# Row sums of a 32 x 512 x 1024 tensor: each load of 16 rows split into a transfer of the even and one of the odd partitions

## Chip, cores, metric

One core of one Trainium2 chip, alone. The metric is device time in microseconds (us), median of several executions.

## The reference

```python
x = np.random.randn(32, 512, 1024).astype(np.float32)   # 67.11 MB
out = np.sum(x, axis=-1).astype(np.float32)             # 16,384 sums
```

## The kernel before

The 16,384 rows are laid out as two blocks, of 112 and of 16 rows for each of the 128 partitions. A tile has 16 rows a partition (128 x 16384 elements), in one of three buffers. VectorE sums a tile in one reduction. SP issues the loads. Seven tiles come from the first block; the second block is cut ever finer (9, 4, 2 rows and one row in two pieces), so that little is left to do when its last bytes land. There, and in the last tile of the first block (7 of its 16 rows), ACT takes part of the rows.

```python
xpool = ctx.enter_context(tc.tile_pool(name="x", bufs=3))
...
        while c < whole:
            m = min(G, whole - c)                       # G = 16
            xt = xpool.tile([P, G * D], F32, tag="xt", name="xt")
            parts = (0, 1, m) if done + c == 0 else (0, m)   # the very first row alone
            for i, k in zip(parts, parts[1:]):
                nc.sync.dma_start(
                    out=xt[:, i * D : k * D], in_=x_b[:, (c + i) * D : (c + k) * D]
                )
            a = ACT_ROWS if done + c + m == full else 0
            rows_dve(xt, res, 0, m - a, c)
            rows_act(xt, res, m - a, a, c + m - a)
            c += m
        if not final:

            for i, k in ((0, 104), (104, P)):
                nc.scalar.dma_start(out=out_b[i:k], in_=res[i:k])
...
    cuts = [0, 9, 13, 15]                               # the last block
    for i, k in zip(cuts, cuts[1:]):
        nc.sync.dma_start(out=xt[:, i * D : k * D], in_=x_b[:, (c + i) * D : (c + k) * D])
```

After compiling, the first `EARLY` loads are moved ahead of the program's starting barrier. (Cuts are marked by "...".)

## Time and profile before

| | before |
|---|---|
| time, median | 162.3 us at first (3 runs); 161.96 to 162.23 in later batches |
| span of the profiled core | 160.4 us |
| VectorE busy | 121.4 us (76%) |
| ACT busy | 17.2 us (11%) |
| DMA engines | 67.18 MB, 419 GB/s over the span |

The two busy shares suggest that no compute engine sets the time; the stretches in the prediction show that the DMA engines do (share 1.00 at 435 GB/s). For the end of the kernel, which the change also touches, here are lines of the timeline of before (start, duration, engine, line, operation, and in brackets the idle time ahead and what ended it):

```profile
147.72 0.99 ACTq L99 DMA_DIRECT2D out_dram<-res  x2
149.07 1.06 ACT L55 ACTIVATE xt<-xt 128x1024 f32<-128x1024 f32 x1 [2.45 <-DMA xt<-in_x_dram]
...
157.48 0.19 ACT L55 ACTIVATION_READ_ACCUMULATOR xt<-xt 128x1 f32 x1
...
158.18 0.35 SPq L128 DMA_DIRECT2D out_dram<-res  x1
```

ACT issues two stores, waits for the nine rows of the last block, and is done 0.5 us before the last store of all is issued.

### The profile page before, as it was taken

The numbers are of one execution on the slowest core, as the hardware profiler recorded it, in microseconds if no ns is written. First come the engines' busy times: TensorE is split into PE (matmuls) and PEld (weight loads), VectorE is DVE, ScalarE is ACT, GpSimd is POOL, SyncE is SP. The second block draws the span as 40 slices with busy tenths as digits, with TensorE's granted clock in tenths as the row PEclk, the third lists the DMA queues.
The fourth block names the chain that finished last, engine by engine and source line by source line (L and its number), as shares of the span: only waits on it lengthen the run. The fifth ranks groups of instructions, "written<-read, shape, count | busy, mean of one in ns | idle before, by whom it ended". The sixth has DMA issues, their size and how long they took to land.

```text
span 160.4 us, 122 instructions
## 1 busy us (share of the span) xinstructions
DVE 121.4 (76%) x17; ACT 17.2 (11%) x31; POOL 0.2 (0%) x4
## 2 busy tenths in 40 slices
DVE  0000059997799959999499994999949998698883
ACT  0000000000000000000000000000000000695892
POOL 0000000000000000000000000000000000000000
DMA  9988996996996996996996996997998999998992
GB/s 376 490 368 368 490 523 261 523 523 261 523 523 261 523 523 261 523 523 261 523 507 278 523 490 294 523 474 310 523 425 359 523 392 392 441 395 369 431 393 79
DMA packets 2169, 67.18 MB, mean 419 GB/s; under 512 B 505, under 2 KB 633, under 8 KB 889
## 3 DMA queue, kind: packets, MB, share of 16 engines
q1 hardware_dynamic: 2016, 67.12, 97.4%
q10 hardware_dynamic: 153, 0.06, 0.1%
HBM read 67.11 MB, written 0.07 MB: 419 GB/s over the span
## 4 chain that ended last, share of the span: by engine, by line
DMA 75%; DVE 22%; SPq 0%; issue 0%; DVEq 0%
DMA xt<-in_x_dram 75%; DVE res L47 21%; DVE pairs L67 1%; SPq L105 0%; DVE seen L123 0%; DVE tail L67 0%; DVEq L136 0%; DVE res L67 0%
## 5 line engine op out<-in xcount | busy, mean ns | idle before, releaser
L47 DVE TENSOR_REDUCE res<-xt 128x16 f32<-128x16384 f32 (+3 forms) x9 | 119.8, 13308 | 35.1 <-DMA xt<-in_x_dram 35.1
L55 ACT ACT_TABLE_LOAD x1 | 1.3, 1283 | 137.9 <-DMA xt<-in_x_dram 137.9
L55 ACT ACTIVATE xt<-xt 128x1024 f32<-128x1024 f32 x15 | 15.6, 1043 | 2.5 <-DMA xt<-in_x_dram 2.5
L55 ACT ACTIVATION_READ_ACCUMULATOR xt<-xt 128x1 f32 x15 | 2.8, 186 | 0.0
L42 DVE MEMSET tail<- 128x1 f32 x1 | 0.1, 59 | 1.3 <-PEq L173 1.3
L67 DVE CUSTOM_DVE_ANT_0 pairs<-xt 128x512 f32<-128x512 f32 x1 | 0.7, 692 | 0.3 <-DMA xt<-in_x_dram 0.3
L67 DVE CUSTOM_DVE_ANT_0 pairs<-tail 128x272 f32<-128x272 f32 (+1 forms) x2 | 0.9, 426 | 0.0
L123 DVE COPY seen<-tail 128x2 f32<-128x2 f32 x1 | 0.2, 168 | 0.0
L67 DVE DVE_READ_ACCUMULATOR2_ANT res<- 128x1 f32 x2 | 0.2, 82 | 0.0
L173 POOL MEMSET const-bfloat16-1.0<- 128x1 bf16 x1 | 0.1, 103 | 0.0
L173 POOL MEMSET const-uint8-127<- 128x1 uint8 x1 | 0.1, 102 | 0.0
L173 POOL MEMSET const-float32-1.0<- 128x1 f32 x1 | 0.1, 100 | 0.0
L173 POOL MEMSET const-float32-0.0<- 128x1 f32 x1 | 0.1, 99 | 0.2 <-issue 0.2
L67 DVE DVE_READ_ACCUMULATOR2_ANT tail<- 128x1 f32 x1 | 0.1, 80 | 0.0
## 6 DMA issues: line engine op xcount, KB each, us to landing
xt<-in_x_dram SPq DMA_DIRECT2D x1, 7680.0 KB
xt<-in_x_dram SPq DMA_DIRECT2D x1, 4608.0 KB, 32.6
xt<-in_x_dram SPq DMA_DIRECT2D x1, 2048.0 KB, 37.1
xt<-in_x_dram SPq DMA_DIRECT2D x1, 1024.0 KB, 39.2
xt<-in_x_dram SPq DMA_DIRECT2D x1, 512.0 KB, 3.6
tail<-in_x_dram SPq DMA_DIRECT2D x1, 272.0 KB, 39.3
tail<-in_x_dram SPq DMA_DIRECT2D x1, 240.0 KB, 39.2
xt<-in_x_dram SPq DMA_DIRECT2D x6, 40.8
```

The lines of the kernel that those rows point to most:

```text
L42: nc.vector.memset(tail[:, CUT + 15 : CUT + 16], 0.0)
L47: nc.vector.tensor_reduce(out=res[:, c : c + n], in_=xt[:, j * D : (j + n) * D].rearrange("p (j d) -> p j d", d=D), axis=X, op=ADD,)
L55: return nc.scalar.activation(out=v, in_=v, func=COPY, accum_out=acc)
L67: nc.vector.tensor_tensor_reduce(out=pairs[:, 0 : h - a], in0=v[:, a:h], in1=v[:, h:b], scale=1.0, scalar=0.0, op0=ADD, op1=ADD, accum_out ...
L123: nc.vector.tensor_copy(out=seen, in_=tail[:, CUT + 14 : CUT + 16])
L173: nc = _bacc.Bacc("TRN2", target_bir_lowering=False, num_devices=1)
```

## The change

Its visible intent: more and smaller transfers, so that a second one is always queued behind the first. Stores of the first block's results become three and stand behind the last loads; three loads are issued ahead of the barrier instead of two.

```diff
-EARLY = 2
+EARLY = 3
@@
-            parts = (0, 1, m) if done + c == 0 else (0, m)
-            for i, k in zip(parts, parts[1:]):
+            parts = [(q, 0, m) for q in (slice(0, P, 2), slice(1, P, 2))]
+            if done + c == 0:
+                parts = [(slice(0, P), 0, 1)] + [(q, 1, m) for q, i, k in parts]
+            for q, i, k in parts:
                 nc.sync.dma_start(
-                    out=xt[:, i * D : k * D], in_=x_b[:, (c + i) * D : (c + k) * D]
+                    out=xt[q, i * D : k * D], in_=x_b[q, (c + i) * D : (c + k) * D]
                 )
@@
         if not final:
-
-            for i, k in ((0, 104), (104, P)):
-                nc.scalar.dma_start(out=out_b[i:k], in_=res[i:k])
+            out_a, res_a = out_b, res
@@ behind the last loads
+    for i, k in ((0, 104), (104, 116), (116, P)):
+        nc.scalar.dma_start(out=out_a[i:k], in_=res_a[i:k])
```

## The prediction

Rival 1, "the clash", is that splitting a tile by partitions slows its packets; no trace of before has a transfer of 64 partitions that lie two apart, and the prediction called this the whole risk. Its figures stand as estimates, from the supposition of half the rate and from the trace: twice 2418 ns is 4.8 us, the 134 us of the split part come a second time (about 296 us in all), half of 435 GB/s is near 220, and half a tile of 19.34 us is the 9.7 that takes the range to 172 us. ("For this" there means a harmless split.) Rival 3 was a fixed cost of every transfer, which the prediction held to be hidden, from the spacing of 19.34 us.

> **What bounds the kernel now.** I read the page's chain of work that ended last first, then its DMA rows, then the windows by stage, then the queue's own waits.
>
> The chain of the kernel before:
>
> ```profile
> DMA 75%; DVE 22%; SPq 0%; issue 0%; DVEq 0%
> DMA xt<-in_x_dram 75%; DVE res L47 21%; DVE pairs L67 1%; SPq L105 0%; DVE seen L123 0%; DVE tail L67 0%; DVEq L136 0%; DVE res L67 0%
> ```
>
> Three quarters of the chain are loads. The 21% of VectorE are two reductions that the chain follows because a later load waits for a buffer which they free. Whether that wait costs time is decided by whether the DMA engines run dry during it. The page's slices of DMA, busy tenths and GB/s, seem to say that they do:
>
> ```profile
> DMA  9988996996996996996996996997998999998992
> GB/s 376 490 368 368 490 523 261 523 523 261 523 523 261 523 523 261 523 523 261 523 507 278 523 490 294 523 474 310 523 425 359 523 392 392 441 395 369 431 393 79
> ```
>
> A 6 after every two 9s looks like a hole at each transfer's end. It is none. A slice is 160.4/40 = 4.01 us. One row of a tile is 16 x 4096 = 65,536 bytes, one packet; the trace's packet records give it a median of 2418 ns, on 16 engines almost in step. So a slice is charged with either one round of packets (16 x 65,536 / 4.01 us = 261 GB/s) or two (523). 523, 523, 261 has the mean 436. The windows by stage, cut where the reductions start, give it without that artefact (columns: stretch and its length, busy us of DVE, ACT and POOL, clock, DMA share, GB/s):
>
> ```profile
> 0.00:2.50 2.50, 0.06 (x1) 0.00 (x0) 0.20 (x4) 1.00 0.55 139
> 21.80:41.10 19.30, 17.22 (x1) 0.00 (x0) 0.00 (x0) 1.00 1.00 435
> 60.50:79.80 19.30, 17.20 (x1) 0.00 (x0) 0.00 (x0) 1.00 1.00 435
> 99.20:118.50 19.30, 17.20 (x1) 0.00 (x0) 0.00 (x0) 1.00 1.01 435
> 137.90:149.10 11.20, 9.76 (x2) 8.69 (x16) 0.00 (x0) 1.00 0.97 408
> 149.10:157.70 8.60, 7.83 (x7) 8.51 (x16) 0.00 (x0) 1.00 0.92 382
> 157.70:160.40 2.70, 0.46 (x3) 0.00 (x0) 0.00 (x0) 1.00 0.03 3
> ```
>
> In the middle the engines have no hole: share 1.00. A tile of 16 rows is 8 packets on each engine, 8 x 2.418 = 19.34 us, and the reductions start 19.3 us apart (21.84, 41.13, 60.48, 79.82, 99.18, 118.53, 137.88 in the timeline). VectorE needs 17.22 of those 19.34 us, so it has 2.1 us to spare for each tile. The kernel is bound by the rate of the 16 engines, 27.1 GB/s each.
>
> How much could any change of the loads win? 67.11 MB at 16 x 27.1 = 433.6 GB/s take 154.8 us; the span is 160.4. Outside stand the first packet's start (1.05 us), the slow first row (its packets take up to 999 ns where 159 is the median, about 1 us), slower packets in the last block (408 and 382 GB/s, about 1 us) and the end after the last landing (2.7 us). The change touches none of these; its aim, the seams between tiles, has nothing to give.
>
> The waits of the SP queue, in which the new waits will stand:
>
> ```profile
> SPq L89 <- DVE res L47: 68.9, 4, 17.3
> SPq L105 <- DVE res L47: 17.2, 1, 17.2
> SPq L105 <- DMA xt<-in_x_dram: 1.8, 1, 1.8
> ```
>
> They cost nothing: the median load needs 40.8 us from issue to landing and itself runs for 19.3, so about one whole load is queued ahead of it.
>
> [...]
>
> **The change, part by part.**
>
> *Loads.* Seven loads (six of 16 rows, one of 15) become fourteen of 64 partitions. The packets stay 65,536 (and 61,440) bytes, 128 for a tile; [...] Added are 7 completion records on each engine; the trace has 9 ns for one: 7 x 9 = 0.06 us on the path. Added are also 7 issues of SP at 328 ns (0.64 the longest): SP is idle for 19 us between loads, so only the start matters. There the third load is issued ahead of the starting barrier, while the first row is in transit; the second transfer has 4 x 2.27 = 9 us of queued work ahead of the third. Nothing on the path.
>
> *Waits.* A reduction waits for two semaphores; both halves pass the same engines one after the other, so the second half lands when the whole tile did. The last loads now wait for semaphores in use: in the compiled order the 4 rows and 2 rows wait for the two halves of tile 5 (landing about 109 and 118.5), the two last pieces for the halves of tile 6 (about 128 and 137.9). The last of these is issued at 138 and is due when the 9 + 4 + 2 rows ahead have passed, about 156.5. 18 us of slack: hidden. Before, the last piece waited for tile 5.
>
> *Stores.* The first block's results go in three transfers (104, 12, 12 partitions) instead of two. Two issues took 0.99 us on ACT's queue from 147.72; a third adds some 0.5, to 149.2, where ACT's next row could start at 149.07. ACT's tail is then up to 0.2 us later, against 0.14 us that it waits before its last row and 0.5 us between its end (157.67) and the last store (158.18): hidden. The third store seems to be there so that the loads of the tail keep their semaphores.
>
> Sum if nothing else happens: 162.3 + 0.06, with a tenth for the waits: 162.4 us.
>
> **The rivals.**
>
> [...]packets of some 4.8 us, not 2.418. For the split part (6 tiles of 19.34 us and 18.1 us, 134 us) that would be 134 us more, about 296 in all. The trace's landings are spread over just 0.56 us, at every tile the same, so engines do run in step. [...]For this speaks only that someone chose even and odd and then took care over the semaphores of the tail, which is not done around a loss of that size. I give the clash, in any form, a quarter.
>
> *2. The seams were real after all,* and a half queued behind each half closes them. Against it: share 1.00 and 19.34 us for eight packets of 2.418. Worth at most the 1 us of the first row or of the tail: 161.3.
>
> [...]
>
> **Range and chances.** Rival 3 and the main line are the same outcome, 162.3 to 162.7, with 161.6 below for luck at start and end. That takes about 0.7. The clash has 0.25, spread from 165 to 296 with no good guide to where. A range that shall hold 8 times in 10 has to take in its mild end: half a tile at half rate is 9.7 us, so up to 172. Faster by over 2% (under 159.1) would have to beat the 154.8 us of data plus the 4.8 us of start (1.05 us, and about 1 us of first row) and end (2.7 us): 0.02. Within 2%: 0.72. Slower: 0.26.
>
> **What would show each step.** Right: packets of 65,536 bytes again at 2418 ns; reductions again 19.3 us apart; the windows' DMA share 1.00 at 435 GB/s; DVE busy 121.4 us; ACT's end and last store no more than 0.3 us later. Rival 1: packets of up to 4.8 us, or in two groups, the windows near 220 GB/s at first, and landings of the 16 engines apart by several us where they were 0.56; the packets of the unsplit first row and last rows as before. Rival 2: no window changes, but the first reduction starts before 21.8. The prediction is wrong if [...]a tail load is issued after the queue has run dry, which would stand as a gap ahead of the 4-row or 2-row reductions (1.44 and 0.46 us of waiting now).

## The result, and the profile after

162.18 us (161.92 to 162.31, 4 runs) against 162.23 us for the kernel before: ratio 0.9997, with a 95% interval of 0.9979 to 1.0016. Nothing changed within noise. A ratio here and below is the mean time of one kernel's fast runs over that of the other's of the same rounds, so it is not quite the ratio of the medians.

The chain of work that ended last, after:

```profile
DMA 73%; DVE 23%; another core or an unknown queue 1%; SPq 1%; issue 0%; DVEq 0%
```

Much the same chain, with loads in front (the unknown queue is one piece of 2.07 us, which the trace does not resolve). The windows of the kernel after, cut at the same times (columns as before):

```profile
0.00:2.50 2.50, 0.06 (x1) 0.00 (x0) 0.20 (x4) 1.00 0.57 139
...
21.80:41.10 19.30, 17.22 (x1) 0.00 (x0) 0.00 (x0) 1.00 1.00 435
...
60.50:79.80 19.30, 17.22 (x1) 0.00 (x0) 0.00 (x0) 1.00 1.00 435
...
99.20:118.50 19.30, 17.22 (x1) 0.00 (x0) 0.00 (x0) 1.00 1.00 435
...
137.90:149.10 11.20, 9.90 (x2) 8.67 (x15) 0.00 (x0) 1.00 0.96 415
149.10:157.70 8.60, 7.88 (x8) 8.23 (x15) 0.00 (x0) 1.00 0.90 372
157.70:160.30 2.60, 0.30 (x2) 0.19 (x2) 0.00 (x0) 1.00 0.04 3
```

The middle is the same to the digit: 435 GB/s at share 1.00. In the trace's records of packets, the 768 packets of 65,536 bytes have the same median, 2418 ns (27.1 GB/s for each of the 16 engines), and the longest of them is 2608 (2493 before). In the same records the second half of the second tile ends 9.7 us after the first half, which is four packets of 2418 ns. The waits of the SP queue did change:

```profile
SPq L93 <- DVE res L47: 69.1, 4, 17.3
SPq L93 <- DMA xt<-in_x_dram: 19.9, 5, 9.0
...
SPq L110 <- DMA xt<-in_x_dram: 18.7, 2, 9.3
SPq L107 <- DVE res L47: 17.3, 1, 17.3
SPq L107 <- DMA xt<-in_x_dram: 2.2, 2, 1.2
```

The row with L110 has grown: the two last pieces now wait 18.7 us in all for semaphores that the halves of the last whole tile still hold, where before they waited 0.2 us (the same line of code was L108 there). Whether this matters is read from the DMA rows and not from the size of the wait: the last piece takes 19.5 us from issue to landing, because 15 rows are queued ahead of it (they had landed by 156.32). And the end of the timeline after:

```profile
147.95 1.40 ACTq L116 DMA_DIRECT2D out_dram<-res  x3
...
149.47 1.06 ACT L55 ACTIVATE xt<-xt 128x1024 f32<-128x1024 f32 x1 [2.60 <-DMA out_dram<-res]
...
157.70 0.19 ACT L55 ACTIVATION_READ_ACCUMULATOR xt<-xt 128x1 f32 x1
...
158.04 0.35 SPq L133 DMA_DIRECT2D out_dram<-res  x1
```

ACT's third store holds it up until 149.47 (149.07 before), and it is done 0.22 us later, at 157.89. That is still 0.15 us ahead of the last store, which goes out at 158.04.

One small thing moved that the prediction did not mention: the third load ahead of the barrier delays the barrier itself, so VectorE's first instruction starts at 2.31 us instead of 1.32. It then waits until 22.00 for data anyway.

### The profile page after: what moved, and what is told of

Read it like the earlier page. It is cut to its first block, busy times and chain, and to the rows that moved or that the text cites. A ratio compares the mean times of both kernels' runs of the same rounds, so it can differ in the third digit from the quotient of the medians.

```text
span 160.3 us, 138 instructions
## 1 busy us (share of the span) xinstructions
DVE 121.5 (76%) x17; ACT 17.1 (11%) x31; POOL 0.2 (0%) x4
## 2 busy tenths in 40 slices
DMA packets 2293, 67.18 MB, mean 419 GB/s; under 512 B 629, under 2 KB 757, under 8 KB 1013
## 4 chain that ended last, share of the span: by engine, by line
DMA 73%; DVE 23%; another core or an unknown queue 1%; SPq 1%; issue 0%; DVEq 0%
DMA xt<-in_x_dram 73%; DVE res L47 21%; DVE pairs L67 1%; SPq L93 1%; DVE seen L128 0%; DVEq L47 0%; DVE tail L67 0%; DVE res L67 0%; DVEq L141 0%
## 6 DMA issues: line engine op xcount, KB each, us to landing
tail<-in_x_dram SPq DMA_DIRECT2D x1, 240.0 KB, 19.5
```

## The experiments

A result of zero has several possible causes: nothing of the change acts; or a gain and a loss cancel; or the risk named in the prediction (the clash: a split by partitions slows the packets) does not exist at all; or it exists, and even and odd partitions happen to avoid it. Nine runs tell these apart. All gave the right result. The expectations name two theories. By theory A the rate depends on which partitions a transfer takes. Its packets of 4.8 us and times of about 290 us are estimates, from twice the 2418 ns of before. (In the forecast for the four transfers, its two outcomes stand one after the other: without a clash and with it.) By theory B the rate does not depend on the partitions.

### The kernel before, a second time

No edit.

> The kernel before, unchanged, for a second trace: how much of the small differences between the two traces (first reduction at 21.84 or 22.00 us, the nine-row packets at a mean of 1405 or 1365 ns, spread of the 16 engines' landings 0.56 or 0.48 us) is chance. If they belong to the change, this run repeats 21.84, 1405 and 0.56 within a few hundredths. If they are chance, at least one of them moves by as much as it did between the two traces. Time 162.2 us either way.

Measured: 162.14 us, ratio 0.9998. First reduction at 22.02 us, mean of the nine-row packets 1367 ns, landings of the 16 engines 0.59 us apart. So the differences of 0.16 us and of 40 ns between the first two traces are chance: this trace of the kernel before has the values of the changed one. The spread of the landings did not move to the changed kernel's 0.48; that it is not the change's either shows in the run with the stores alone, whose unsplit loads land within 0.43 to 0.50 us. These differences are not explained further.

### Halves instead of even and odd

```diff
-            parts = [(q, 0, m) for q in (slice(0, P, 2), slice(1, P, 2))]
+            parts = [(q, 0, m) for q in (slice(0, 64), slice(64, P))]
```

> As the changed kernel, but the two transfers take partitions 0 to 63 and 64 to 127. Theory A ([...]even/odd partitions cost nothing[...]):[...] packets slow down to at least 4.8 us and the kernel takes 290 us or more;[...] packets of up to 9.7 us, up to 560 us.[...] Theory B ([...]the 27.1 GB/s are the engines' own): packets stay at 2.42 us, 162.3 us.

Measured: 308.78 us, ratio 1.904. The windows of this run, each one tile long:

```profile
42.00:82.40 40.40, 17.18 (x1) 0.00 (x0) 0.00 (x0) 1.00 1.00 208
122.90:163.40 40.50, 17.26 (x2) 0.00 (x0) 0.00 (x0) 1.00 1.00 207
204.00:244.40 40.40, 17.14 (x1) 0.00 (x0) 0.00 (x0) 1.00 1.00 208
```

The DMA share is 1.00, as in the kernel before: all 16 engines are busy all the time, at half the rate. A share of 1.00 says that the engines hold packets, not that they move them at full speed; the GB/s beside it say that (208 here, 435 before). A packet of 65,536 bytes has a median of 5118 ns, and the 16 landings of a transfer stay 0.9 us apart, so all 16 engines take part, in step. Theory B falls: the engines move 27.1 GB/s each with even and odd partitions (65,536 bytes in 2418 ns), and 12.8 with the halves (in 5118). The very same edit with other slices nearly doubles the time, so the change did carry the risk. Theory A said this in advance, except for the size: not 4.8 us but 5.1, so a packet takes 2.1 times as long, not 2. Why it does is not shown. Packets of 9.7 us (an estimate for a worse case: four times 2418 ns) did not appear.

### Four transfers a tile

```diff
-            parts = [(q, 0, m) for q in (slice(0, P, 2), slice(1, P, 2))]
+            parts = [(slice(r, P, 4), 0, m) for r in range(4)]
```

> As the changed kernel, but four transfers a tile, of the partitions that are 0, 1, 2, 3 modulo 4. [...]packets 2.42 us, 162.4 us (14 more completion records of 9 ns are 0.13 us). [...]about 290 us in step. Theory B: 162.4 us. If a transfer has a cost of its own on the path, it shows here three times as large as in the changed kernel: over 0.5 us more would need such a cost of over 25 ns.

Measured: 162.29 us against 162.12, ratio 1.0005 (0.9988 to 1.0022), packets 2418 ns, the longest 2434. Again no clash (2418 ns in the changed kernel too), and three times as many extra transfers as in the changed kernel cost at most a few tenths of a us. A fixed cost for each transfer, if any is on the path, is too small to see here.

### Eight transfers a tile

```diff
-            parts = [(q, 0, m) for q in (slice(0, P, 2), slice(1, P, 2))]
+            parts = [(slice(r, P, 8), 0, m) for r in range(8)]
```

> As the changed kernel, but eight transfers a tile, of the partitions that are r modulo 8. [...]Theory A: packets of 4.8 us as long as the engines are in step, about 290 us; [...]Theory B: packets 2.42 us, 162.3 us plus 49 completion records of 9 ns (0.4 us).

Measured: 309.56 us, ratio 1.909, median packet 5105 ns. A window of one tile:

```profile
42.00:82.40 40.40, 17.19 (x1) 0.00 (x0) 0.00 (x0) 1.00 1.01 208
```

Split by 2 or by 4 nothing happens (2418 ns); split by 8 the rate is halved (208 GB/s for 435). So being spread is not enough: 64 partitions 2 apart and 32 that lie 4 apart run at full rate, 16 that lie 8 apart and 64 neighbours do not. The size of a transfer in bytes does not tell these runs apart: the quarter is smaller than the half and runs at full rate. What does tell them apart was not shown: theory A expected the slow packets of the halves and of the eight transfers, but from a mechanism that no record shows. In every run the rows that are read go with the partitions that are written, so not even the reading and the writing side were set apart.

### Engines put out of step

This tells whether the full rate of the even/odd transfers hangs on the engines being in step (theory A2) or not (theory A1). The first forecast is that of A1, and the second that of A2, whose 2.5 to 4.8 us are an estimate: up to twice the 2418 ns.

```diff
             if done + c == 0:
-                parts = [(slice(0, P), 0, 1)] + [(q, 1, m) for q, i, k in parts]
+                uneven = [slice(0, P, 16), slice(8, P, 16)]
+                uneven += [slice(r, P, 8) for r in (2, 4, 6)] + [slice(1, P, 2)]
+                parts = [(slice(0, P), 0, 1)] + [(q, 1, 8) for q in uneven] + [(q, 8, m) for q, i, k in parts]
```

> The changed kernel with the engines put out of step on purpose: rows 1 to 7 of the first tile come in six uneven transfers, of which the first two (8 partitions each) give packets to eight engines only; from row 8 on all is as in the changed kernel. [...]the 768 packets of 65,536 bytes stay at 2418 ns, though the 16 landings of a transfer now lie some 2 to 5 us apart, where they were 0.5. Cost only at the start and the end, 164 to 169 us. [...]packets of 2.5 to 4.8 us all through the run, and 175 us or more.

Measured: 170.47 us, ratio 1.052; a little over the stated 169, because the uneven transfers themselves run slower than I had reckoned: their packets of 28,672 bytes take a median of 2082 ns and up to 3558, where 1062 is my estimate of the undisturbed time (28,672 bytes at 36.76 ps and 8.7 ns a packet, from the packet times given with the split by rows), and the first reduction starts at 30.01 us, 8.0 later than in the changed kernel. After that nothing is lost, as three windows show:

```profile
40.00:59.40 19.40, 17.20 (x2) 0.00 (x0) 0.00 (x0) 1.00 1.00 432
79.00:98.40 19.40, 17.26 (x2) 0.00 (x0) 0.00 (x0) 1.00 1.00 432
118.00:137.40 19.40, 17.20 (x2) 0.00 (x0) 0.00 (x0) 1.00 1.00 432
```

The 16 landings now lie 1.86 us apart, a little less than the 2 to 5 expected, in two groups of eight, and stay so from the first tile to the last. The 768 packets take 2418 to 2429 ns, where theory A2 asked for 2.5 to 4.8 us. The landings inside the groups differ by up to 0.18 and 0.64 us, and no packet is stretched by more than 11 ns. So theory A2 fails, and A1 holds: out of step or in step, the packets keep their time for the length of the run. Which engine took which packets was not seen, as the packet records do not name engines.

### Eight transfers in another order

```diff
-            parts = [(q, 0, m) for q in (slice(0, P, 2), slice(1, P, 2))]
+            parts = [(slice(r, P, 8), 0, m) for r in (0, 4, 1, 5, 2, 6, 3, 7)]
```

Two outcomes were named: the clash wears off, or it stays.

> As the run with eight transfers a tile, but in the order 0, 4, 1, 5, 2, 6, 3, 7[...]. [...]packets come down to 2.42 us after some tiles and the time is 165 to 200 us. [...]packets stay near 5.1 us and the time near 309 us.

Measured: 302.5 us (one run, state unknown); the 768 packets of 65,536 bytes took 4902 to 5029 ns. The clash did not wear off. The first and the last landing of a transfer lie 2.47 us apart, half a packet, but that is one engine alone: the other 15 land within 1.00 us. I cannot say why the packets come down from 5105 to 4909 ns and no further; this stays open. None of three clashing kernels came out below 302 us. That speaks against the mild clash, for whose sake the prediction's range went up to 172 us, but only for these three splits.

### The stores alone

To the kernel before only this was done:

```diff
-            for i, k in ((0, 104), (104, P)):
-                nc.scalar.dma_start(out=out_b[i:k], in_=res[i:k])
+            out_a, res_a = out_b, res
@@ behind the last loads
+    for i, k in ((0, 104), (104, 116), (116, P)):
+        nc.scalar.dma_start(out=out_a[i:k], in_=res_a[i:k])
```

> The kernel before with nothing of the change but its stores: three transfers (104, 12, 12 partitions) issued behind the last loads. If the zero of the whole change is the sum of a gain and a loss, this part is off from 1 by itself. By the prediction it is hidden: 162.2 us, ratio 0.998 to 1.002.

Measured: 161.98 us against 161.96, ratio 0.9999 (0.9981 to 1.0016). No hidden gain or loss in this part. Its trace shows that moving the stores is enough to lengthen a wait: the two last pieces wait 19.7 us in all (0.2 before), and that too costs nothing.

### Split by rows instead of partitions

```diff
-            parts = [(q, 0, m) for q in (slice(0, P, 2), slice(1, P, 2))]
+            parts = [(slice(0, P), 0, 8), (slice(0, P), 8, m)]
             if done + c == 0:
-                parts = [(slice(0, P), 0, 1)] + [(q, 1, m) for q, i, k in parts]
+                parts = [(slice(0, P), 0, 1), (slice(0, P), 1, 8), (slice(0, P), 8, m)]
```

> The change's number of transfers and waits, but split by rows and not by partitions: two transfers of 8 rows from all 128 partitions. Packets are half as large and twice as many. From the packet times (2418 ns for 65,536 bytes, 1364 for 36,864: 36.76 ps a byte and 8.7 ns a packet) 8 more packets a tile on each engine cost 0.07 us, over seven tiles 0.5 us: 162.7 us, ratio 1.003. If there were a gap at the seam of tiles that a second queued transfer closes, this split would close it too, and the time would fall below 162.1.

Measured: 162.47 us against 161.96, ratio 1.0028 (1.0010 to 1.0046); 1.003 was expected from 8.7 ns for each extra packet (the two packet times give 8.9, and here two packets of 32,768 bytes take 2 x 1214 = 2428 ns for 2418). So the extra packets account for the whole of it, and the extra transfers have no cost that shows; the even/odd split leaves the number of packets of 65,536 bytes at 768. This run also settles what the 9-9-6 pattern of the page's slices was. Its DMA row:

```profile
DMA  9899999999999999999999999999999999998991
```

With packets half as long the "holes" are gone, and the kernel is not faster but 0.5 us slower. They were an artefact of packets that are long beside the slice (2.4 of 4.0 us).

### Two stores in the changed kernel

```diff
-    for i, k in ((0, 104), (104, 116), (116, P)):
+    for i, k in ((0, 104), (104, P)):
```

> The changed kernel with two stores for the first block (104 and 24 partitions, as before) in place of three. The semaphores of the last loads then shift by one: the last piece waits for the first half of the last whole tile (landing about 128) and not for the second (138). If these waits are hidden, as the prediction says, and the third store only keeps the order of semaphores, the time is that of the changed kernel, 162.0 to 162.4 us, ratio 0.998 to 1.002. If the later wait or the third issue costs something, this run is faster by it, at most some 0.2 us.

Measured: 162.15 us against 162.08, ratio 1.0002 (0.9985 to 1.0019). The two last pieces wait 10.0 us in all here, against 18.7, and ACT's first row behind the stores starts at 149.07 us, against 149.47. So neither the later wait of the last piece nor the third store costs anything that can be seen in the time.

### All runs

| run | us | ratio to before | packet of 65,536 bytes, median ns | partitions of a transfer of such rows |
|---|---|---|---|---|
| changed kernel | 162.18 | 0.9997 | 2418 | 64, 2 apart |
| before again | 162.14 | 0.9998 | 2418 | 128 |
| halves | 308.78 | 1.904 | 5118 | 64 neighbours |
| four transfers | 162.29 | 1.0005 | 2418 | 32, 4 apart |
| eight transfers | 309.56 | 1.909 | 5105 | 16, 8 apart |
| out of step | 170.47 | 1.052 | 2420.5 | 64, 2 apart (uneven in part of the first tile) |
| eight, other order | 302.5 | one run | 4909 | 16, 8 apart |
| stores alone | 161.98 | 0.9999 | 2418 | 128 |
| by rows | 162.47 | 1.0028 | none; 1214 for 32,768 | 128 |
| two stores | 162.15 | 1.0002 | 2418 | 64, 2 apart |

## Why the prediction was right

**The time.** 162.4 us was forecast, 162.18 measured, with "within 2%" at 0.72. The argument for it holds: the DMA engines have no hole at the seams of tiles, so there was nothing to win. Shown by the windows of both kernels, and by the split in rows, which closes the apparent holes and gains nothing. Two slips in the sums change nothing: 162.3 + 0.06 and a tenth are 162.46, not 162.4, and the first packet starts at 1.01 us, not 1.05.

**Loads.** Packets of 2418 ns and reductions 19.3 us apart, as forecast. Four transfers a tile confirm that completion records and issues cost too little to see; the forecast 0.06 us for them is below what these runs can resolve. One cost was mis-sized: SP's issue of a load of 64 partitions takes a median of 589 ns (588 in the halves), where the prediction took the 328 ns of the loads before. With some 19 us for two of them, this is hidden all the same.

**Waits.** Right in kind and place: the last piece is issued at about 138 us (the two issues stand at 128.36 to 138.36 in the timeline) and lands 19.5 us later. The rows ahead of it had landed by 156.32, where I had said 156.5. The run with two stores moves the wait and changes nothing.

**Stores.** Right, with less to spare than said: ACT ended 0.22 us later (0.2 forecast), and its slack ahead of the last store shrank from 0.5 to 0.15 us. That the 0.2 was met is partly luck: the first row behind the stores started 0.40 us later (149.07 to 149.47), not 0.13 as reckoned, and the wait before the last row took up part of it; some 0.2 of the 0.40 is this trace's own lateness (its stores begin at 147.95, those of before at 147.72 and, in the second trace, 147.89). The stores alone have ratio 0.9999.

**Rival 1.** This is where the document learns most. The clash is real for other splits, and its size was nearly right: 296 us estimated, 302.5 to 309.6 measured in three kernels that do have it, with packets 2.03 to 2.12 times as long (4909 to 5118 ns for 2418) and not 2 times. The sign that it gave, landings several us apart, did not come with the clash (0.9 us in the halves). What the prediction could not know is whether 64 partitions that lie 2 apart clash. Its three chances in four for a harmless split rested on a guess at someone's care and on no trace, so on this point it was lucky. The runs show that this split is harmless (2418 ns) and that the halves and the eight transfers are not; which rule separates them was not shown, and no record names the engine. One thing of the prediction's treatment found no support. It let a clash wear off; in the three clashing kernels it did not (windows of the halves at 208, 207 and 208 GB/s, the same in the eight transfers; no packet under 4902 ns in the other order), so the outcomes between 165 and 290 us, for whose sake the range went up to 172, have nothing measured behind them.

**Rivals 2 and 3** did not occur: neither a gain at the start (first reduction at 22.00 us, and 22.02 in the second trace of before) nor a cost for each transfer that these runs can resolve. (No run here shows such a cost by itself; the unbroken spacing of 19.3 us, for eight packets of 2418 ns, shows that none stands on the path.)

## What to carry to other kernels

Before splitting a transfer, look at GB/s in windows of one tile, not at the busy digits of the slices: with packets of 2.4 us in slices of 4.0 the digits showed holes that were not there, and in the halves the windows' DMA share showed full use (1.00) at half the rate. Where the engines already ran at 27.1 GB/s each, a split had nothing to gain; whether it is harmless or doubles the time hangs on which partitions go together. Here those 2 or 4 apart kept their packets at 2418 ns, and 64 neighbours or those 8 apart took 5118 and 5105; the rule behind it was not shown, so time a split before you rely on it, and do not cut its packets without need (half as long cost 0.3% here). A wait in the queue's list need not cost anything: 18.7 us of it were hidden here, because 15 rows of loads stood ahead of the load that waited.
